# A decoder trunk on one core: the sums of the first two inner tiles' weights, and three low parts, move from VectorE to GpSimd

## The chip, the core and the metric

The kernel runs on one core of one Trainium2 chip. A core has a matrix engine (TensorE, PE in the profile, with its weight loads shown apart as PEld), VectorE (DVE), ScalarE (ACT), GpSimd (POOL) and SyncE (SP), which here only issues DMAs. Each engine takes its instructions strictly in order; what couples engines are semaphores that an instruction waits on before it starts. The metric is the device time of one execution in microseconds (us), as the median of several runs.

## The reference, cut to what matters

The reference is one inference step of a small decoder: one layer with a state-space mixer, one with differential attention, and after each of them a gated feed-forward network with a short convolution. The part that matters here is that network:

```python
def conv_ffn(x, buf, w_up, conv_w, conv_b, w_down):
    h = x @ w_up                               # (tokens, 1024) @ (1024, 5632)
    hp = jnp.concatenate([buf, h], axis=1)
    hc = conv_b + conv_w[0]*hp[:, 0:L] + conv_w[1]*hp[:, 1:1+L] + conv_w[2]*hp[:, 2:2+L]
    gate, val = jnp.split(hc, 2, axis=-1)
    return (gelu(gate) * val) @ w_down
```

It is computed for 1024 prompt tokens and 64 sample tokens together (1088 columns), once per layer, so twice in the program. Everything is float32, and the result has to be close to float32.

## The kernel before

**Three products for one.** A float32 operand is split in two: a high part, rounded by ScalarE (`A.copy`, line 144), and a low part, which is the operand minus the high part (line 145, VectorE). A product is then three matmuls, lines 809 to 811: high by high, low by high, high by low. `split_evac` (line 141) makes both parts. The names `whi` and `wlo` are the parts of weights, `xT_hi` and `xT_lo` those of the transposed activations.

**The up projection** is `ffn_up`, line 1090. It runs over 22 inner tiles f, each with 128 gate columns and 128 value columns of the weights. The first 768 tokens are multiplied by a scheme with seven products in place of eight (Strassen's, in Winograd's form), which needs sums of the weights' four quarters and sums of the activations' four quarters. `inputs(f)`, line 1099, prepares one inner tile: two DMAs bring the gate and the value weights into two `raw` tiles (line 1104), four sums s1 to s4 of 128 by 512 elements (lines 1109 to 1112) go into two `xr` tiles, and four calls of `split_evac` (line 1116) make the high and low parts of the gate weights, of the two `xr` tiles, and of the value weights. `raw` has two buffers and `xr` has two: the next inner tile's loads wait until the last reader of this one's `raw` tiles is done, and the first sums of a phase wait until the `xr` tiles of the phase before have been read.

**What comes ahead of it.** The activations of the up projection are made by the stage before it, tile of 128 tokens by tile: a residual addition (line 854), a second normalisation (line 864) with a Newton iteration on 128 by 1 elements for the inverse root (lines 120 to 134), then transposes on PE (line 870) and a `split_evac`. For three pairs of token tiles the sums of the activations (lines 911 to 914, `Combos.pair`) are made on VectorE before the transposes. The stage before is the gated output of the mixer (`glu`, first layer) or the attention's output projection (`o_proj`, second layer). So at the start of an up projection VectorE has the tail of the last stage and the head of the next at the same time.

**What sets the order.** The program is written in a straight line; a scheduler then orders each engine's instructions by an estimate of when each would be ready. The order so found is fixed when the program is built. SyncE's queue is in order too. Within a phase, the `acc` tiles (14 buffers) are used in turn, so a tile's first writer may have to wait for the last reader of an older one: in `inputs`, GpSimd clears two columns of each new `acc` tile (line 1121) and copies a few more (line 1122).

Of the kernel before, what the change touches and what calls it, by code (L numbers as in the profile page):

```python
# [10 lines left out]
F32 = mybir.dt.float32  # L11
# [4 lines left out]
ALU = mybir.AluOpType  # L16
# [57 lines left out]
def trunk_kernel(ctx, tc, I, O):  # L74
    nc = tc.nc
    V = nc.vector
    A = nc.scalar
    PE = nc.tensor
    GP = nc.gpsimd
    uid = [0]  # L80

    def nm(s):
        uid[0] += 1
        return f"{s}_{uid[0]}"
# [53 lines left out]
    xh = xpool.tile([P, KT, T], F32R, tag="xT_hi", name="xT_hi")  # L138
    xl = xpool.tile([P, KT, T], F32R, tag="xT_lo", name="xT_lo")

    def split_evac(hi_ap, lo_ap, ps_ap, scale=None):

        if scale is None:
            A.copy(hi_ap, ps_ap)  # L144
            V.tensor_tensor(lo_ap, ps_ap, hi_ap.bitcast(F32), ALU.subtract)  # L145
        else:
            A.mul(hi_ap, ps_ap, scale)
            V.scalar_tensor_tensor(lo_ap, ps_ap, scale, hi_ap.bitcast(F32), op0=ALU.mult, op1=ALU.subtract)
# [626 lines left out]
    def wslot(name, dtype=F32):  # L775

        c = pools["wc"] = (pools.get("wc", -1) + 1) % NWX
        return pools["w"].tile([P, 1024], dtype, tag=f"wx{c}", name=nm(name), bufs=1)
# [19 lines left out]
    def slot(tag, shape=None, dtype=F32):  # L798

        al = {"gx": "acc", "post": "acc", "junk": "gr"}  # L800
        shp, bufs = {"acc": ([P, 2 + SEQ + NB * 10], NACC), "gx": ([P, 4, 2 * P], NACC), "gr": ([P, 512], NGR),
                     "xr": ([P, D], 2), "junk": ([P, D], NGR), "post": ([P, D], NACC),
                     "cvo": ([P, 4, 18], 2), "cpar": ([P, 2 * NF, 20], 1), "ss": ([P, 1], 4)}[tag]
        tag = al.get(tag, tag)
        return pools["ph"].tile(shape or shp, dtype, tag=tag, name=nm(tag), bufs=bufs)
# [67 lines left out]
    def tail_b(y, tt, scale=None):  # L873

        t0, n = tokens(tt)
        for h in range(2):
            split_evac(xh[:, 4 * h : 4 * h + 4, t0 : t0 + n], xl[:, 4 * h : 4 * h + 4, t0 : t0 + n],
                       transposed(y[:, 512 * h : 512 * h + 512], n), scale)
# [6 lines left out]
    class Combos:  # L885
# [11 lines left out]
        def store(self, s, t, c0):  # L897
            k = 0
            while k < 4:
                n = min(3 - (4 * s + k) % 3, 4 - k)  # L900
                hi, lo = [self.view(s, part, k, n)[:, :, c0 : c0 + P] for part in range(2)]
                split_evac(hi, lo, t[:, k : k + n])
                k += n

        def pair(self, ya, yb, tt):

            t0 = tt * P
            tr = lambda y: transposed(y, P)
            t1, t2, t3, t4 = [slot("gr") for _ in range(4)]
            a, b = slice(0, 512), slice(512, D)  # L910
            V.tensor_tensor(t1, yb[:, a], ya[:, a], ALU.subtract)
            V.tensor_tensor(t3, yb[:, b], yb[:, a], ALU.subtract)
            V.tensor_tensor(t2, yb[:, b], t1, ALU.subtract)
            V.tensor_tensor(t4, ya[:, b], t2, ALU.subtract)
            split_evac(xh[:, 0:4, t0 : t0 + P], xl[:, 0:4, t0 : t0 + P], tr(t1))
            split_evac(xh[:, 4:8, t0 : t0 + P], xl[:, 4:8, t0 : t0 + P], tr(yb[:, b]))
            for s, t in enumerate((t2, t3, t4)):
                self.store(s, tr(t), t0 - HT)
# [171 lines left out]
    def ffn_up(i, down):  # L1090
# [8 lines left out]
        def inputs(f):  # L1099
            raws, hbs = [], []  # L1100
            for s in range(2):
                raw = pools["w"].tile([P, 1024], F32, tag="raw", name=nm("raw"), bufs=2)
                rv = u3(raw)
                nc.sync.dma_start(rv, wv[:, :, s * FF + f * P : s * FF + (f + 1) * P])
                raws.append(rv)
            a11, a12, a21, a22 = [r[:, 4 * k : 4 * k + 4] for r in raws for k in range(2)]
            s12, s34 = u3(slot("xr")), u3(slot("xr"))
            s1, s2, s3, s4 = [t[:, 4 * k : 4 * k + 4] for t in (s12, s34) for k in range(2)]
            V.tensor_tensor(s1, a21, a22, ALU.add)
            V.tensor_tensor(s2, s1, a11, ALU.subtract)  # L1110
            V.tensor_tensor(s3, a11, a21, ALU.subtract)
            V.tensor_tensor(s4, a12, s2, ALU.subtract)
            ws = []
            for r in (raws[0], s12, s34, raws[1]):
                hi, lo = u3(wslot("whi", F32R)), u3(wslot("wlo", F32R))
                split_evac(hi, lo, r)
                ws.append((hi, lo))
            for s in range(2):
                hb = slot("acc")
                hs = hb[:, 2 + SEQ :].rearrange("p (b r) -> p b r", r=10)  # L1120
                GP.memset(hb[:, 0:2], 0.0)
                GP.tensor_copy(hs[:, :, 0:2], cp[:, s * NF + f, 4:NPAR].rearrange("p (b r) -> p b r", r=2))
                hbs.append(hb)
            st[f] = ws, hbs, []
# [93 lines left out]


        inputs(0)  # L1220
        g = first(0)
        for _ in range(3):
# [8 lines left out]
        for f in range(NAHEAD, NF):  # L1231
            inputs(f)
            if f == NF - 1:
                down.begin()
            for s, _ in enumerate(first(f)):
                rest(f, s)
                conv(f, s)
            outputs(f)
# [865 lines left out]
```

## Time and profile before

| what | value |
|---|---|
| median of 3 runs | 2679.99 us (2677.94 to 2682.68) |
| the profiled execution | 2684.83 us, of which 2682.9 us are the span of the profile |
| busy share of PE, DVE, ACT, POOL | 93%, 73%, 47%, 24% |
| granted TensorE clock, mean | 0.976 of full speed |
| first up projection | about 436 to 930 us |
| second up projection | about 1906 to 2410 us |

A row of the page or of a timeline gives the start in us, the duration in us, the engine, the line, the operation, and what is written and read. Where an engine was idle ahead of the instruction, a bracket gives for how long and what released it. A row with "x2" at its end holds two instructions.

### The profile page before, as it was taken

The page shows a single profiled execution, that of the slowest core. Times are in us where ns is not written, and L with a number is a line of the kernel's source. Part 1 is how long each engine was busy: PE and PEld are TensorE (multiplying, and loading weights), DVE is VectorE, ACT ScalarE, POOL GpSimd, SP SyncE. Part 2 cuts the span into 40 slices and gives each one's busy share as a digit, 9 for nine tenths or more (in the row PEclk, how much of TensorE's full clock was granted, in tenths as well). Part 3 has the DMA queues.
Part 4 walks back from the last instruction along what each step waited for, and adds up shares of the span by engine and source line. Part 5 has one row for each costly group of instructions (what it writes and reads, how often), then busy time and mean ns, then how long its engine had stood idle before and what let it go on. Part 6 is the DMA issues. An engine that isn't in the chain of part 4 may idle for free.

```text
span 2682.9 us, 39622 instructions
## 1 busy us (share of the span) xinstructions
PE 2500.6 (93%) x14234; PEld 2203.5 (82%) x14234; DVE 1963.5 (73%) x3683; ACT 1270.9 (47%) x2559; POOL 657.3 (24%) x1062
## 2 busy tenths in 40 slices
PE   3778998999999989999999899989799999998997
PEld 2777887999999967778777788877699999996775
DVE  7994358777777789984232688875877777778999
ACT  6763334444444454354322677764544444444432
POOL 3220030111111175501201222113011111137661
PEclk9999998999999999999999899999899999999998
DMA  5443233222222233444646433335322222233334
GB/s 145 99 98 88 85 124 124 65 83 74 74 74 74 89 116 92 127 145 166 204 157 211 104 79 95 97 105 171 115 69 79 74 74 74 74 104 107 94 102 145
DMA packets 265688, 286.77 MB, mean 107 GB/s; under 512 B 42268, under 2 KB 212564, under 8 KB 265492
## 3 DMA queue, kind: packets, MB, share of 16 engines
q1 hardware_dynamic: 261892, 273.55, 33.0%
q0 software_dynamic: 3088, 9.77, 1.7%
q8 instruction: 113, 1.85, 0.3%
q10 hardware_dynamic: 512, 0.92, 0.1%
q14 instruction: 83, 0.68, 0.1%
HBM read 193.58 MB, written 70.93 MB: 99 GB/s over the span
## 4 chain that ended last, share of the span: by engine, by line
PE 58%; DVE 13%; DMA 4%; issue 3%; ACT 3%; POOL 2%; SPq 0%; DVEq 0%; POOLq 0%; ACTq 0%
PE mm L809 17%; PE mm L810 17%; PE mm L811 17%; DVE acc L1428 2%; DMA gr<-gd 1%; DVE xT_lo L145 1%; DVE S L1898 1%; PE mm L1417 1%; ACT S L1902 1%; DVE wst L145 1%; DVE xT_hi L145 1%; DVE acc L854 1%; PE mm L1436 1%; PE tr L870 1%; PE mm L1926 1%
## 5 line engine op out<-in xcount | busy, mean ns | idle before, releaser
L809 PE MATMUL mm<-xT_hi,whi 128*128 128x384 f32 (+1 forms) x1408 | 457.0, 325 | 2.0 <-ACT acc L1146 1.8
L810 PE MATMUL mm<-xT_lo,whi 128*128 128x384 f32 (+1 forms) x1408 | 456.3, 324 | 1.6 <-DVE xT_lo L145 1.6
L811 PE MATMUL mm<-xT_hi,wlo 128*128 128x384 f32 (+1 forms) x1408 | 454.2, 324 | 0.0
L809 PEld LDWEIGHTS mm<-xT_hi,whi 128*128 128x128 f32 x1408 | 265.4, 189 | 3.8 <-ACT acc L1146 2.4
L810 PEld LDWEIGHTS mm<-xT_lo,whi 128*128 128x128 f32 x1408 | 265.7, 189 | 2.4 <-DVE xT_lo L145 2.3
L811 PEld LDWEIGHTS mm<-xT_hi,wlo 128*128 128x128 f32 x1408 | 265.4, 189 | 0.8
L1195 POOL COPY cvo<-acc 128x2 f32<-128x2 f32 x88 | 53.3, 606 | 818.5 <-ACT acc L1178 818.5
L809 PE MATMUL mm<-whi,xT_hi 128*128 128x512 f32 x608 | 243.9, 404 | 4.9 <-ACT whi L792 4.7
L1192 DVE SCALAR_TENSOR_TENSOR acc<-acc,cpar,acc 128x1104 f32<-128x1104 f32 x176 | 240.0, 1385 | 4.7 <-ACT acc L1190 4.6
L810 PE MATMUL mm<-wlo,xT_hi 128*128 128x512 f32 x608 | 241.9, 398 | 0.1
L811 PE MATMUL mm<-whi,xT_lo 128*128 128x512 f32 x608 | 241.7, 399 | 0.0
L144 ACT CAST whi<-raw 128x1024 fp32r<-128x1024 f32 x88 | 92.5, 1051 | 253.5 <-PE mm L811 245.2
L1428 DVE TENSOR_TENSOR acc<-mm,acc 128x512 f32<-128x512 f32 x279 | 184.7, 680 | 9.8 <-PE mm L811 9.3
L145 DVE TENSOR_TENSOR wlo<-raw,whi 128x1024 fp32r<-128x1024 f32 x88 | 107.7, 1224 | 107.0 <-PE mm L810 91.6
L809 PE MATMUL mm<-acc,whi 128*128 128x384 f32 x528 | 179.1, 339 | 0.0
L811 PE MATMUL mm<-acc,wlo 128*128 128x384 f32 x528 | 178.7, 339 | 0.0
L810 PE MATMUL mm<-acc,whi 128*128 128x384 f32 x528 | 178.3, 338 | 0.0
L809 PEld LDWEIGHTS mm<-whi,xT_hi 128*128 128x128 f32 x608 | 115.6, 191 | 36.2 <-ACT whi L792 5.6
L810 PEld LDWEIGHTS mm<-wlo,xT_hi 128*128 128x128 f32 x608 | 114.7, 189 | 27.8 <-DVE wlo L793 0.8
L811 PEld LDWEIGHTS mm<-whi,xT_lo 128*128 128x128 f32 x608 | 114.4, 188 | 27.6 <-issue 0.8
L1190 ACT ACTIVATE acc<-acc,cpar 128x1104 f32<-128x1104 f32 x88 | 114.1, 1311 | 18.1 <-DVE acc L1161 11.9
L145 DVE TENSOR_TENSOR wlo<-xr,whi 128x1024 fp32r<-128x1024 f32 x88 | 107.6, 1223 | 16.7 <-ACT whi L144 8.6
(572 smaller groups left out, 6255.9 us busy)
## 6 DMA issues: line engine op xcount, KB each, us to landing
raw<-in_w_up_dram SPq DMA_DIRECT2D x88, 512.0 KB
gd<-acc SPq DMA_DIRECT2D x44, 552.0 KB
raw<-in_w_down_dram SPq DMA_DIRECT2D x44, 512.0 KB
gr<-gd SPq DMA_DIRECT2D x80, 256.0 KB
raw<-in_glu_w_dram SPq DMA_DIRECT2D x40, 256.0 KB
acc<-in_cache_k_dram SPq DMA_DIRECT2D x16, 512.0 KB
acc<-in_cache_v_dram SPq DMA_DIRECT2D x16, 512.0 KB
xj<-in_x_prompt_dram SPq DMA_DIRECT2D x8, 512.0 KB
```

Source lines behind the costliest of these rows:

```text
L144: A.copy(hi_ap, ps_ap)
L145: V.tensor_tensor(lo_ap, ps_ap, hi_ap.bitcast(F32), ALU.subtract)
L809: PE.matmul(out, lh, rh, start=start, stop=False, **kw)
L810: PE.matmul(out, lh, rl, start=False, stop=False, **kw)
L811: PE.matmul(out, ll, rh, start=False, stop=stop, **kw)
L854: V.scalar_tensor_tensor(y[:, hs], y[:, hs], r[0:n], xr[0:n, hs], op0=ALU.mult, op1=ALU.add)
L870: PE.transpose(ps[:, c * n : (c + 1) * n], y[:, c * P : (c + 1) * P], ident[0:n, 0:n])
L1190: A.activation(hc, hb[:, 2 : 2 + TG], AF.Identity, bias=cp[:, ft, 3:4], scale=cp[:, ft, 2:3])
L1192: V.scalar_tensor_tensor(hc, hb[:, tap : tap + TG], cp[:, ft, tap : tap + 1], hc, op0=ALU.mult, op1=ALU.add)
L1195: GP.tensor_copy(co[:, 0:2], hb[:, SEQ : SEQ + 2])
L1417: PE.matmul(pa[h], lt, wt[:, h * 512 : (h + 1) * 512], start=st and j == 0, stop=sp and j == len(seq) - 1)
L1428: V.tensor_tensor(a, ps, a, ALU.add)
```

## The change

For the first two inner tiles of each up projection the four sums of weights are given to GpSimd, and for the first inner tile three of the four low parts as well (those of the two sum tiles and of the value weights; the low part of the gate weights stays on VectorE). Both up projections have it, so 16 sums and 6 low parts move in all. No value that is computed changes, and the other 20 inner tiles are as before. The file grows by two lines, so that what is line 1109 before is line 1111 after, and so on from there; line 145 stays.

```diff
-    def split_evac(hi_ap, lo_ap, ps_ap, scale=None):
+    def split_evac(hi_ap, lo_ap, ps_ap, scale=None, on=V):
 
         if scale is None:
             A.copy(hi_ap, ps_ap)
-            V.tensor_tensor(lo_ap, ps_ap, hi_ap.bitcast(F32), ALU.subtract)
+            on.tensor_tensor(lo_ap, ps_ap, hi_ap.bitcast(F32), ALU.subtract)
...
-            V.tensor_tensor(s1, a21, a22, ALU.add)
-            V.tensor_tensor(s2, s1, a11, ALU.subtract)
-            V.tensor_tensor(s3, a11, a21, ALU.subtract)
-            V.tensor_tensor(s4, a12, s2, ALU.subtract)
+
+            E = GP if f < 2 else V
+            E.tensor_tensor(s1, a21, a22, ALU.add)
+            E.tensor_tensor(s2, s1, a11, ALU.subtract)
+            E.tensor_tensor(s3, a11, a21, ALU.subtract)
+            E.tensor_tensor(s4, a12, s2, ALU.subtract)
             ws = []
-            for r in (raws[0], s12, s34, raws[1]):
+            for j, r in enumerate((raws[0], s12, s34, raws[1])):
                 hi, lo = u3(wslot("whi", F32R)), u3(wslot("wlo", F32R))
-                split_evac(hi, lo, r)
+                split_evac(hi, lo, r, on=GP if f == 0 and j else V)
```

Since the scheduler orders all engines anew, instructions that the diff doesn't touch move too.

**VectorE and GpSimd, start of the first up projection.** raw_4230 and raw_4232 are the gate and value weights of the first inner tile, xr_4234 and xr_4235 its sums, raw_4503 and raw_4505 the weights of the second inner tile, gr_4291 to gr_4294 the activations' sums. VectorE before:

```order
L854 SCALAR_TENSOR_TENSOR acc_4136<-acc_4136,rr_4175,xr_4167 128x1024
L864 SCALAR_TENSOR_TENSOR acc_4071<-acc_4071,rr_4191,acc_2343 128x1024
L1111 TENSOR_TENSOR xr_4235<-raw_4230,raw_4232 128x512
L1112 TENSOR_TENSOR xr_4235<-raw_4230,xr_4234 128x512
L911 TENSOR_TENSOR gr_4291<-acc_4006,acc_3956 128x512
L912 TENSOR_TENSOR gr_4293<-acc_4006 128x512
L120 TENSOR_SCALAR rv_4218<-ss_4216 128x1
L913 TENSOR_TENSOR gr_4292<-acc_4006,gr_4291 128x512
L145 TENSOR_TENSOR wlo_4249<-xr_4235,whi_4248 128x1024
```

and now:

```order
L854 SCALAR_TENSOR_TENSOR acc_4136<-acc_4136,rr_4175,xr_4167 128x1024
L864 SCALAR_TENSOR_TENSOR acc_4071<-acc_4071,rr_4191,acc_2343 128x1024
L911 TENSOR_TENSOR gr_4291<-acc_4006,acc_3956 128x512
L912 TENSOR_TENSOR gr_4293<-acc_4006 128x512
L120 TENSOR_SCALAR rv_4218<-ss_4216 128x1
L913 TENSOR_TENSOR gr_4292<-acc_4006,gr_4291 128x512
L123 TENSOR_SCALAR rr_4220<-rv_4218 128x1
L914 TENSOR_TENSOR gr_4294<-acc_3956,gr_4292 128x512
```

What left VectorE stands on GpSimd, whose queue held only the two clears and two copies here:

```order
L145 TENSOR_TENSOR wlo_4253<-raw_4232,whi_4252 128x1024
L1111 TENSOR_TENSOR xr_4234<-raw_4232 128x512
L1112 TENSOR_TENSOR xr_4234<-xr_4234,raw_4230 128x512
L1123 MEMSET acc_4256 128x2
L1124 COPY acc_4256<-cpar_2673 128x8x2
L145 TENSOR_TENSOR wlo_4245<-xr_4234,whi_4244 128x1024
L1113 TENSOR_TENSOR xr_4235<-raw_4230,raw_4232 128x512
L1114 TENSOR_TENSOR xr_4235<-raw_4230,xr_4234 128x512
L1123 MEMSET acc_4259 128x2
L1124 COPY acc_4259<-cpar_2673 128x8x2
L145 TENSOR_TENSOR wlo_4249<-xr_4235,whi_4248 128x1024
```

The activations' sums now follow the normalisations with no weight work between, and GpSimd has eleven rows where it had four.

**ScalarE, the same place.** whi_4248 is the high part of xr_4235, whi_4513 that of the second inner tile's gate weights, acc_4259 the copy of the first product out of its accumulator, which PE waits for. Before:

```order
L144 CAST whi_4248<-xr_4235 128x1024
L144 CAST xT_hi<-tr_4299 128x4x128
L144 CAST whi_4513<-raw_4503 128x1024
L1146 COPY acc_4259<-mm_4262 128x384
L144 CAST xT_hi<-tr_4306 128x4x128
L144 CAST acc_3409<-tr_4313 128x3x128
```

and now:

```order
L144 CAST xT_hi<-tr_4299 128x4x128
L144 CAST whi_4248<-xr_4235 128x1024
L144 CAST xT_hi<-tr_4306 128x4x128
L1148 COPY acc_4259<-mm_4262 128x384
L144 CAST whi_4513<-raw_4503 128x1024
L144 CAST acc_3409<-tr_4313 128x3x128
```

The copy now stands ahead of the second inner tile's cast, but still behind the cast of xr_4235; the cast of the second inner tile stands ahead of acc_3409, the first activation sum.

**VectorE, start of the second up projection.** acc_18615 is a token tile whose second normalisation (L864) PE waits for; wlo_19052 is the low part of the second inner tile's gate weights, raw_19043 that tile's value weights. Before:

```order
L145 TENSOR_TENSOR wlo_19052<-raw_19041,whi_19051 128x1024
L134 SCALAR_TENSOR_TENSOR rr_18743<-rs_18742,rr_18743 128x1
L1109 TENSOR_TENSOR xr_19045<-raw_19043 128x512
L145 TENSOR_TENSOR acc_17917<-tr_18784,acc_17913 128x2x128
L130 SCALAR_TENSOR_TENSOR rs_18806<-rr_18807,rv_18805 128x1
L1111 TENSOR_TENSOR xr_19046<-raw_19041,raw_19043 128x512
L145 TENSOR_TENSOR acc_17917<-tr_18793,acc_17913 128x128
L864 SCALAR_TENSOR_TENSOR acc_18615<-acc_18615,rr_18743,acc_17778 128x1024
```

and now:

```order
L134 SCALAR_TENSOR_TENSOR rr_18743<-rs_18742,rr_18743 128x1
L130 SCALAR_TENSOR_TENSOR rs_18806<-rr_18807,rv_18805 128x1
L864 SCALAR_TENSOR_TENSOR acc_18615<-acc_18615,rr_18743,acc_17778 128x1024
L134 SCALAR_TENSOR_TENSOR rr_18807<-rs_18806,rr_18807 128x1
L145 TENSOR_TENSOR acc_17917<-tr_18784,acc_17913 128x2x128
L145 TENSOR_TENSOR wlo_19052<-raw_19041,whi_19051 128x1024
```

The normalisation that stood behind the low part of the second inner tile now stands ahead of it.

## The prediction

> **What bounds the kernel now.** First the page's span and busy times, then equal windows of 50 us (columns: window, its length, busy PE with its instructions, PEld, DVE, ACT, POOL, granted clock, DMA share, GB/s).
>
> ```profile
> span 2682.9 us, 39622 instructions
> PE 2500.6 (93%) x14234; PEld 2203.5 (82%) x14234; DVE 1963.5 (73%) x3683; ACT 1270.9 (47%) x2559; POOL 657.3 (24%) x1062
> ...
> 400.00:450.00 50.00, 39.50 (x195) 31.79 (x194) 44.85 (x121) 23.29 (x55) 3.39 (x8) 0.94 0.42 141
> 500.00:550.00 50.00, 50.00 (x305) 49.83 (x305) 37.56 (x43) 22.71 (x31) 4.36 (x16) 1.00 0.24 77
> 1900.00:1950.00 50.00, 37.41 (x203) 35.84 (x204) 42.79 (x102) 24.20 (x41) 5.50 (x12) 0.83 0.29 95
> ```
>
> Inside an up projection (500 to 550) PE is never idle, so that nothing is to be had there; at its two beginnings PE lacks 10.5 and 12.6 us of 50 and DVE is the fullest engine. Only there does the change count. What PE waits for, between 430 and 480 and between 1880 and 1960 (total, times, longest):
>
> ```profile
> PE tr L870 <- DVE gr L911: 9.7, 1, 9.7
> PE mm L809 <- ACT acc L1146: 1.1, 1, 1.1
> ...
> PE tr L870 <- DVE acc L864: 11.7, 2, 6.8
> ```
>
> So the instructions that matter are L911 in the first layer, L864 in the second, and L1146 between the halves of the first product. DVE ahead of L911:
>
> ```profile
> 433.79 1.23 DVE L145 TENSOR_TENSOR wlo<-raw,whi 128x1024 fp32r<-128x1024 f32 x1
> 436.21 0.69 DVE L145 TENSOR_TENSOR xT_lo<-tr,xT_hi 128x512 fp32r<-128x512 f32 x1
> 444.44 1.28 DVE L854 SCALAR_TENSOR_TENSOR acc<-acc,rr,xr 128x1024 f32<-128x1024 f32 x1
> 447.44 0.69 DVE L1112 TENSOR_TENSOR xr<-raw,xr 128x512 f32<-128x512 f32 x1
> 448.04 0.69 DVE L911 TENSOR_TENSOR gr<-acc,acc 128x512 f32<-128x512 f32 x1
> ```
>
> From 433.79 to 448.04 DVE runs without a pause. A sum costs it 0.60 (447.44 to 448.04), a low part about 1.2.
>
> **The price on POOL.** The same shapes on POOL elsewhere in this program (shortest, median, longest, in ns):
>
> ```profile
> L1298 POOL TENSOR_TENSOR xr<-raw,xr x36: 1286/1487/2328, 935.1 to 2601.9; 128x512 f32<-128x512 f32 x36
> L1804 POOL TENSOR_TENSOR qwl<-qraw,qwh x8: 2352/2369/2541, 1473.7 to 1701.2; 128x1024 fp32r<-128x1024 f32 x8
> ```
>
> So 1.29 a sum and 2.37 a low part, twice DVE's. POOL has room (3.39 and 5.50 of 50). But do the two engines run side by side?
>
> ```profile
> L134 DVE SCALAR_TENSOR_TENSOR rr<-rs,rr x204: 139/159/973, 8.6 to 2677.4; 128x1 f32<-128x1 f32 x69, 128x8 f32<-128x8 f32 x12, 128x2 f32<-128x2 f32 x12, 64x1 f32<-64x1 f32 x9
> ...
> 1209.91 1.89 POOL L791 TENSOR_TENSOR raw<-raw,kvg 128x1024 f32<-128x1024 f32 x1 [33.75 <-DMA raw<-in_w_k_dram]
> 1210.85 0.97 DVE L134 SCALAR_TENSOR_TENSOR rr<-rs,rr 128x1 f32<-128x1 f32 x1
> ...
> 955.14 4.44 POOL L1298 TENSOR_TENSOR xr<-raw 128x512 f32<-128x512 f32 x1 [4.37 <-DVE xT_hi L145]
> 956.15 1.28 DVE L145 TENSOR_TENSOR xT_hi<-xr,xT_hi 128x512 fp32r<-128x512 f32 x2
> ...
> 2601.91 1.49 POOL L1298 TENSOR_TENSOR xr<-raw,xr 128x512 f32<-128x512 f32 x1
> 2602.16 1.87 DVE L1428 TENSOR_TENSOR acc<-mm,acc 128x512 f32<-128x512 f32 x3
> ```
>
> They don't. At 1210.85 a DVE instruction whose line has a median of 0.16 lasts 0.97, its longest: until just the end of POOL's (1211.80). At 955.14 POOL's sum of 1.29 lasts 4.44 while DVE runs subtractions of two buffers in SBUF one behind another: POOL gets in when DVE pauses. At 2602.16 DVE reads `mm`, the accumulator, and three of them keep their 0.62 beside POOL's sum. I read: DVE with two sources in SBUF and POOL exclude each other; a DVE row with a source in the accumulator (L1428, xT_lo) doesn't.
>
> [...]
>
> **First layer.** Six of DVE's instructions ahead of L911 go: two low parts and four sums, 2 x 1.23 + 4 x 0.60 = 4.9; alone, L911 would start at 443.1. On POOL stand, ready in the same stretch, two low parts and two sums: 2 x 2.37 + 2 x 1.29 = 7.3. Two rows like that at 436.21 cover 1.4 of it, and 5.9 hold DVE. L911 comes at 448.04 - 4.9 + 5.9 = 449.0, 1.0 later. Lower bound: none holds it, -4.9.
>
> Now what is queued behind. The other two sums (L1111, L1112) write an `xr` tile that the last L854 still reads; that starts 3.6 before L911 in the rows above, 2.4 once the two sums between have gone, so it ends near 447.8. Then DVE has L864, L911 and L912 in a row, to 450.2, and POOL gets in at the small gap behind: 1.29, L913's 0.60, 1.29, so that L1112 ends near 453.5, where it was 448.1. On it hang, in this order, ACT's cast of that tile and (behind it in ACT's queue) the copy L1146 that PE waits for; and SP's load of the second tile.
>
> ```profile
> 448.87 1.09 PE L870 MATMUL tr<-ident,gr 128*128 128x128 f32 x4 [9.73 <-DVE gr L911]
> 452.81 0.69 PE L809 MATMUL mm<-xT_hi,whi 128*128 128x384 f32 x1 [1.14 <-ACT acc L1146]
> 457.40 0.42 PE L809 MATMUL mm<-acc,whi 128*128 128x384 f32 x1
> ...
> 451.33 1.04 ACT L144 CAST whi<-raw 128x1024 fp32r<-128x1024 f32 x1 [0.75 <-DMA raw<-in_w_up_dram]
> 452.29 0.47 ACT L1146 COPY acc<-mm 128x384 f32<-128x384 f32 x1
> ```
>
> ACT: cast 1.04, an xT_hi of half its size 0.5, copy 0.47: from 453.5 to 455.5, and PE goes on at 455.7 in place of 452.81: **+2.9**. The second tile's load, issued at L1112's end (447.60 before) and landing 3.7 later (451.33), lands near 457.2; its cast and that of the activation sum behind it end at 458.8, while PE asks for the latter at 455.7 + (457.40 - 452.81) = 460.3. It stays hidden with 1.5 to spare; without that cover each us of delay counts. Bounds of this layer: -4.9 (no exclusion at all) and +6.1 (each of the two sums takes 4.44, like that at 955.14).
>
> **Second layer.**
>
> ```profile
> 1905.81 1.94 PE L870 MATMUL tr<-ident,acc 128*128 128x128 f32 x8 [6.82 <-DVE acc L864]
> 1928.38 1.92 PE L870 MATMUL tr<-ident,acc 128*128 128x128 f32 x8 [4.84 <-DVE acc L864]
> 1933.17 1.07 PE L870 MATMUL tr<-ident,acc 128*128 128x128 f32 x8
> ...
> 1917.02 0.69 DVE L1112 TENSOR_TENSOR xr<-raw,xr 128x512 f32<-128x512 f32 x1
> 1922.80 1.05 ACT L144 CAST whi<-raw 128x1024 fp32r<-128x1024 f32 x1 [3.19 <-DMA raw<-in_w_up_dram]
> 1923.88 1.23 DVE L145 TENSOR_TENSOR wlo<-raw,whi 128x1024 fp32r<-128x1024 f32 x1 [2.72 <-ACT whi L144]
> 1926.95 1.28 DVE L864 SCALAR_TENSOR_TENSOR acc<-acc,rr,acc 128x1024 f32<-128x1024 f32 x1
> ```
>
> Up to the middle the exchange is as above: a low part at 2.37 for 1.23, mostly beside DVE's work, +0.7 at the first gap, then two sums at 1.29 for 0.60, +1.4, and +0.4 of another low part: PE is 2.5 late. The second gap, 4.84, is of another kind: L864 stood in DVE's queue behind the second inner tile's low part, which idled 2.72 for ACT's cast, which idled 3.19 for the DMA. In the new order L864 stands ahead of it. So PE, which came free at 1928.38 - 4.84 = 1923.5, comes at 1926.0 and goes straight on: -2.4. The next token tile's L864 is now the one behind that low part. POOL's L1112, held by the clear of `acc` and by DVE, ends near 1921 (1917.7 before); load 5.1 (1917.7 to 1922.80), cast 1.05, low part 1.23, a little of DVE's other work, L864: about 1930.3. These transposes start at 1930.4 in place of 1933.17: **-2.8**. Bounds: -4.84 - 1.1 (both waits go, the six sums cost nothing) and +2.5 (the second gap only moves).
>
> **Clock.** After the gap:
>
> ```profile
> 1928.00:1931.00 3.00, 2.62 (x11) 2.65 (x12) 3.00 (x8) 2.05 (x3) 0.00 (x0) 0.57 0.00 0
> 1931.00:1934.00 3.00, 3.00 (x19) 2.70 (x18) 2.78 (x6) 0.16 (x1) 0.00 (x0) 0.86 0.59 175
> ...
> 2423.30:2425.70 2.40, 0.00 (x1) 0.00 (x0) 2.40 (x5) 0.00 (x0) 2.40 (x1) 0.99 0.91 267
> 2427.00:2430.00 3.00, 3.00 (x8) 2.32 (x8) 1.80 (x2) 1.48 (x3) 2.92 (x3) 0.50 0.66 204
> ```
>
> The 4.84 cost 3 x 0.43 + 3 x 0.14 = 1.7 more in clock. A stall of about 1.4 stays in my account (1929.0 to 1930.4), shorter than the 2.40 that still cost the clock at 2423; I credit half, **-0.9**.
>
> [...]
>
> **Sum**, against the profiled execution's own 2684.83: +2.9 - 2.8 - 0.9 = -0.8, 2684.0; this execution lies 4.84 above the median, so about **2679** in the median's terms. A measurement of this kernel can tell some 0.2% (5.4 us) from no change, so below 2674.6 is faster and above 2685.4 slower.
>
> **Rivals.**
> A, the engines hardly hold each other: DVE finishes its head early. For it: POOL is nearly empty, and much of DVE here is 128 by 1 work between dependent steps, with gaps that POOL can use; against it, 1210.85. First layer -4.4, second -4.84 - 1.7 - 1.1 = -7.6: 2668.
> B, slower: the two late sums starve. Each waits for a pause of DVE as at 955.14 (4.44 - 1.29 = 3.2); L1112 ends at 447.8 + 2 x 4.44 = 456.7, ACT's cast holds L1146 and PE goes on 6.1 later; in the second layer the same 3 us push the load and eat the 2.8, and the gap with its clock stays: 2686. It decides when L1112 ends after 456; from 454.3 on the sum turns to a loss. For it, those 4.44; against it, that DVE's row here has 128 by 1 pauses.
> C, nothing comes of it, because the waits for DMA and ACT set both places whatever DVE does: 2680. For it, the bracket at 1922.80; against it, the 9.7 for L911.
>
> **Chances.** Forecast 0.43, A 0.31, B 0.21, C 0.05. The forecast's own range, from its bounds, is 2673 to 2686: of its 0.43, 0.03 lies below 2674.6 and 0.03 above 2685.4; of B 0.04 lies within. So faster 0.31 + 0.03 = 0.34; slower 0.17 + 0.03 = 0.20; no change 0.46. For 8 in 10 the range reaches to both rivals: 2668 to 2687.
>
> **What will show it.** First layer: the gap ahead of L870 ends near 450, the second half of the product starts near 455.7, the late sum ends near 453.5, and rows of DVE with two SBUF sources (L130, L134, L854) are longer where POOL works. Second layer: no 4.84 ahead of `tr` at 1926, and the last token tile's transposes at 1930.4. I am wrong by A if DVE's rows keep their lengths beside POOL's and L911 comes near 444; by B if `whi` or the load is PE's last releaser past 456; altogether if PE's idle time changes outside these two beginnings.

## The result

The changed kernel takes 2689.81 us (median of 7 runs, 2686.83 to 2694.56); the kernel before, on the same chip, 2682.45 us (7 runs, 2677.86 to 2685.75). The ratio is 1.0031, with a 95% interval of 1.0022 to 1.0040: slower by some 8 us (the two medians are 7.4 apart). The prediction was 2679 and "no change" as the likeliest, with 2687 as the upper end of its range. The sign is that of rival B, the mechanism is not.

**The profile after.** Busy times, then the 50 us windows of the two beginnings (columns as before):

```profile
PE 2497.0 (93%) x14234; PEld 2200.9 (82%) x14234; DVE 1973.5 (73%) x3661; ACT 1271.1 (47%) x2559; POOL 663.0 (25%) x1084
...
400.00:450.00 50.00, 37.63 (x181) 29.79 (x180) 46.75 (x114) 23.42 (x52) 14.41 (x11) 0.87 0.46 153
1900.00:1950.00 50.00, 35.71 (x186) 33.41 (x185) 43.57 (x86) 21.38 (x40) 21.23 (x17) 0.83 0.32 105
```

VectorE has 22 instructions fewer and is busy for longer: 1973.5 us, where it was 1963.5. In the first window it went from 44.85 to 46.75 with some operations gone. The rows below show why: a row's duration contains the time for which GpSimd holds the instruction up (L911 at 443.80 lasts 1.75, and 0.69 before), so the work that left came back as waiting. What PE waits for, in the windows 430 to 480 and 1880 to 1960:

```profile
PE tr L870 <- DVE gr L911: 7.3, 1, 7.3
PE mm L810 <- DVE xT_lo L145: 3.3, 1, 3.3
PE mm L810 <- DVE acc L145: 1.7, 1, 1.7
...
PE tr L870 <- DVE rr L134: 6.9, 1, 6.9
PE mm L809 <- ACT acc L144: 3.2, 1, 3.2
PE tr L870 <- DVE rr L123: 3.0, 1, 3.0
```

The stall of 4.84 us in the second layer has gone, as forecast, and so has that for L1146 in the first. In their place stand three new ones: 1.7, 3.0 and 3.2. Two lines need care. The 3.3 for xT_lo (0.3 before) stands right ahead of the 7.3 in PE's queue; together they are 10.6, where it was 10.0 before, so most of it has only moved from one to the other. And the 6.9 put down to L134 is the old 6.8 for L864: L864 ends at 1907.04, a short L134 right behind it at 1907.18, and PE goes on at 1907.19.

**First layer, by rows.** GpSimd, VectorE and PE of the changed kernel:

```profile
429.63 2.38 POOL L145 TENSOR_TENSOR wlo<-raw,whi 128x1024 fp32r<-128x1024 f32 x1 [31.64 <-DVE rr L134]
442.77 2.24 POOL L1113 TENSOR_TENSOR xr<-raw,raw 128x512 f32<-128x512 f32 x1 [2.06 <-DVE acc L854]
444.97 1.72 POOL L1114 TENSOR_TENSOR xr<-raw,xr 128x512 f32<-128x512 f32 x1
452.81 1.28 POOL L1113 TENSOR_TENSOR xr<-raw,raw 128x512 f32<-128x512 f32 x1
...
429.46 2.56 DVE L130 SCALAR_TENSOR_TENSOR rs<-rr,rv 128x1 f32<-128x1 f32 x2
443.80 1.75 DVE L911 TENSOR_TENSOR gr<-acc,acc 128x512 f32<-128x512 f32 x1
452.90 1.20 DVE L134 SCALAR_TENSOR_TENSOR rr<-rs,rr 128x1 f32<-128x1 f32 x1
...
445.70 1.09 PE L870 MATMUL tr<-ident,gr 128*128 128x128 f32 x4 [7.33 <-DVE gr L911]
450.18 0.67 PE L809 MATMUL mm<-xT_hi,whi 128*128 128x384 f32 x1
458.13 0.44 PE L810 MATMUL mm<-acc,whi 128*128 128x384 f32 x1 [1.74 <-DVE acc L145]
```

A Newton step on 128 by 1 elements, 0.15 us alone, lasts until GpSimd's low part or sum beside it ends: two of them 2.56 beside the low part at 429.63, one 1.20 beside the sum at 452.81. L911, 0.69 before, lasts 1.75, since GpSimd's L1113 has its turn first, up to 445.01. The stall of 1.74 is the low part of an activation sum, which stands behind the Newton steps that the second tile's sums hold.

**Second layer, by rows.** PE, then VectorE and GpSimd:

```profile
1915.90 1.09 PE L870 MATMUL tr<-ident,gr 128*128 128x128 f32 x4 [3.03 <-DVE rr L123]
1918.90 0.69 PE L809 MATMUL mm<-xT_hi,whi 128*128 128x384 f32 x1 [0.20 <-ACT acc L1148]
1922.49 0.34 PE L809 MATMUL mm<-acc,whi 128*128 128x384 f32 x1
1927.59 0.60 PE L870 MATMUL tr<-ident,acc 128*128 128x128 f32 x4
1932.35 0.66 PE L809 MATMUL mm<-acc,whi 128*128 128x384 f32 x1 [3.19 <-ACT acc L144]
1936.02 1.03 PE L870 MATMUL tr<-ident,acc 128*128 128x128 f32 x8
...
1913.50 2.26 DVE L911 TENSOR_TENSOR gr<-acc,acc 128x512 f32<-128x512 f32 x1
1925.74 2.35 DVE L134 SCALAR_TENSOR_TENSOR rr<-rs,rr 128x1 f32<-128x1 f32 x1
1928.35 2.05 DVE L145 TENSOR_TENSOR wlo<-raw,whi 128x1024 fp32r<-128x1024 f32 x1
1930.32 1.21 DVE L130 SCALAR_TENSOR_TENSOR rs<-rr,rv 128x1 f32<-128x1 f32 x1
...
1912.87 2.34 POOL L145 TENSOR_TENSOR wlo<-xr,whi 128x1024 fp32r<-128x1024 f32 x1 [1.16 <-DVE rv L120]
1924.88 3.19 POOL L145 TENSOR_TENSOR wlo<-xr,whi 128x1024 fp32r<-128x1024 f32 x1 [3.37 <-ACT whi L144]
1929.28 2.24 POOL L1113 TENSOR_TENSOR xr<-raw,raw 128x512 f32<-128x512 f32 x1
```

The stall of 3.03 is L911 waiting out the low part at 1912.87. The stall of 3.19 is the low part of an activation sum that stood behind three held rows: a Newton step at 1925.74, 2.2 us longer than alone beside the first inner tile's last low part (1924.88), and 1928.35 and 1930.32, some 0.8 and 1.0 longer beside the second inner tile's sums.

### The profile page after: what moved, and what is told of

Same layout as the page of the kernel before. It is cut to its first block, busy times and chain, and to the rows that moved or that the text cites. A ratio compares the mean times of both kernels' runs of the same rounds, so it can differ in the third digit from the quotient of the medians.

```text
span 2687.6 us, 39649 instructions
## 1 busy us (share of the span) xinstructions
PE 2497.0 (93%) x14234; PEld 2200.9 (82%) x14234; DVE 1973.5 (73%) x3661; ACT 1271.1 (47%) x2559; POOL 663.0 (25%) x1084
## 4 chain that ended last, share of the span: by engine, by line
PE 63%; DVE 19%; DMA 5%; ACT 5%; issue 4%; POOL 3%; SPq 0%; DVEq 0%; ACTq 0%; POOLq 0%
PE mm L809 18%; PE mm L810 18%; PE mm L811 18%; DMA gr<-gd 2%; DVE acc L1430 2%; DVE xT_lo L145 2%; DVE S L1900 1%; POOL rs L126 1%; DVE acc L854 1%; ACT S L1904 1%; DVE xT_hi L145 1%; PE mm L1419 1%; PE mm L1928 1%; PE mm L1438 1%; DVE wst L145 1%
## 5 line engine op out<-in xcount | busy, mean ns | idle before, releaser
L1900 DVE CUSTOM_DVE_ANT_0 S<-mm,tb 128x512 f32<-128x512 f32 (+3 forms) x192 | 101.5, 552 | 22.4 <-PE mm L1898 18.9
```

The lines of the kernel that those rows point to most:

```text
L1900: V.tensor_tensor_reduce(S_[j][:, k0 : k0 + w], ps[:, 0:w], H["tb"][:, b0 : b0 + w], 0.125, -3e38, ALU.add, ALU.max, mx[:, j, c : c + 1])
```

## The experiments

The profiles all hold 14,234 matrix instructions, so the time at which PE starts its nth can be compared between them, whatever the order of the rest. The table gives, worked out from the traces, how long PE takes from its 2077th to its 3169th (399.7 to 599.6 us in the first profile of the kernel before: the first beginning), from the 10173rd to the 10726th (1889.7 to 1999.7: the second), in between, and from there to its last. The ratio is to the kernel before, with its 95% interval.

| kernel | ratio | first beginning | between | second beginning | behind it |
|---|---|---|---|---|---|
| before, the first profile | | 199.9 | 1290.2 | 110.0 | 667.6 |
| before, again | | 198.4 | 1289.7 | 110.1 | 667.6 |
| the change | 1.0031 [1.0022, 1.0040] | 203.8 | 1292.5 | 112.2 | 668.7 |
| first projection only | 1.0017 [1.0008, 1.0025] | 204.4 | 1286.6 | 110.6 | 668.2 |
| second projection only | 1.0015 [1.0006, 1.0024] | 199.4 | 1289.0 | 111.9 | 668.5 |
| memsets in place of reads | 1.0005 [0.9996, 1.0013] | 192.9 | 1294.5 | 102.7 | 678.4 |
| memsets, again | | 192.4 | 1293.7 | 103.6 | 680.2 |
| moved work left out | 0.9975 [0.9964, 0.9985] | 194.0 | 1297.8 | 104.1 | 669.3 |
| change, Newton steps with one source | 1.0014 [1.0005, 1.0023] | 200.7 | 1287.7 | 110.3 | 666.5 |
| before, Newton steps with one source | 1.0044 [1.0031, 1.0057] | 200.4 | 1287.4 | 110.7 | 675.3 |
| sums only | 1.0021 [1.0012, 1.0029] | 200.8 | 1292.9 | 107.9 | 667.7 |
| low parts only | 1.0034 [1.0023, 1.0045] | 203.3 | 1295.8 | 111.8 | 667.7 |
| second projection, first tile only | 1.0011 [1.0002, 1.0019] | 198.5 | 1292.3 | 110.9 | 669.5 |
| second projection, second tile's sums only | 1.0011 [1.0001, 1.0020] | 198.3 | 1289.8 | 113.1 | 670.0 |
| one low part only | 1.0009 [0.9999, 1.0018] | 198.2 | 1289.3 | 111.5 | 668.7 |
| three raw buffers, ten slots | 0.9961 [0.9948, 0.9974] | 197.5 | 1289.8 | 107.0 | 665.3 |
| the change, three raw buffers, ten slots | 1.0006 [0.9996, 1.0015] | 201.3 | 1286.4 | 117.5 | 665.2 |
| ten slots | 1.0001 [0.9992, 1.0010] | 198.3 | 1287.6 | 107.0 | 670.8 |

Where its order is as before, the first beginning takes 198.2 to 199.9 in six profiles, and the second 110.0 to 110.6 in three: a single profile is good to about 1.7 and 0.6 us. Between them the six profiles whose order is as before up to the second beginning lie from 1289.0 to 1292.3.

### Each projection by itself

```diff
-            E = GP if f < 2 else V
+            E = GP if f < 2 and i == 0 else V
...
-                split_evac(hi, lo, r, on=GP if f == 0 and j else V)
+                split_evac(hi, lo, r, on=GP if f == 0 and j and i == 0 else V)
```

> The change in the first up projection only. Theory L, from the traces (there the change's execution goes from 4.9 us ahead at the row L864 to 0.9 ahead after the beginning): 3 to 5 us above the kernel before. If the difference of the medians is from elsewhere: within 1 us.

The same with `i == 1`:

> The change in the second up projection only. Theory L, from the traces (1.3 us behind at L2025, 4.8 behind after the beginning): 2.5 to 4.5 us above the kernel before. By the prediction as made: 3.7 below.

Measured 1.0017 and 1.0015, some 4 us each; together that is the loss of the whole change. The first beginning is 4.5 to 6.2 us longer than in the six profiles with its order unchanged, the second 1.3 to 1.9 than in the three. So there is a loss in both beginnings. In the second the profile shows less than the median (1.9 of 4.0, whose interval begins at 1.6). The prediction of -3.7 for the second (-2.8, and -0.9 of clock) is refuted by a run of its own.

### The exclusion: memsets in place of reads

```diff
-            E.tensor_tensor(s1, a21, a22, ALU.add)
...
+            if f < 2:
+                for s, p, q in ((s1, a21, a22), (s2, s1, a11), (s3, a11, a21), (s4, a12, s2)):
+                    GP.tensor_tensor(s[:, :, 0:1], p[:, :, 0:1], q[:, :, 0:1], ALU.subtract)
+                    for _ in range(3):
+                        GP.memset(s, 0.0)
```

and the three low parts alike.

> Each of the 22 moved operations is replaced on GpSimd by the same operation on a 128 by 4 or 128 by 8 slice (so that it waits for the same data) and three memsets of its whole tile, which take longer than the operation (three of 0.46 or 0.92 us by the two memsets of 128 by 1024 in 1.84) but read nothing; the sums and low parts are left out. Theory L (GpSimd's reads and VectorE's two-source operations exclude each other, and that exclusion is the loss): the loss goes, VectorE's rows keep their lengths, 4 to 12 us below the kernel before. Rival O (GpSimd's results come late, or the new order of the rows is bad): the loss stays, 4 to 9 us above the kernel before.

At the two beginnings theory L holds, by more than its own upper end: 192.9 and 102.7, that is 7.0 and 7.3 us below the first profile of the kernel before, and 5.5 and 7.4 below the second. GpSimd is as busy, and VectorE doesn't notice:

```profile
431.42 2.98 POOL L148 MEMSET wlo<- 128x1024 f32 x3
431.19 0.35 DVE L130 SCALAR_TENSOR_TENSOR rs<-rr,rv 128x1 f32<-128x1 f32 x2
```

Two Newton steps take 0.35 beside a memset; beside the low part at 429.63 of the changed kernel two took 2.56. The wait of PE for the pair sums (L916 here), 7.3 in the changed kernel, falls to 3.7:

```profile
PE tr L875 <- DVE gr L916: 3.7, 1, 3.7
```

But the median is that of the kernel before, not 4 to 12 us below: 10.8 us are given back behind the second beginning (678.4 against 667.6). To see whether that was the single execution, the kernel was profiled once more:

> The kernel with memsets in place of the moved operations, one more profile: its gain of 6.8 and 4.9 us at the two beginnings stays within 1 us if it belongs to the order and the lack of exclusion; what is given back in the second down projection (7.8 us) stays if it belongs to the order there, and goes if it was the single execution.

By the table's marks the gains are 7.5 and 6.4 us, within 1 us of the 7.0 and 7.3 of its first profile (the 6.8, 4.9 and 7.8 of the expectation aren't taken at these marks), and 680.2 stays too. So the loss behind belongs to this kernel's order, which differs in the later tiles of the second up projection and in the down projection behind it. Which row does it was not found.

### What VectorE's relief is worth

```diff
-            s12, s34 = u3(slot("xr")), u3(slot("xr"))
+            s12, s34 = raws if f < 2 else (u3(slot("xr")), u3(slot("xr")))
...
-            on.tensor_tensor(lo_ap, ps_ap, hi_ap.bitcast(F32), ALU.subtract)
+            if on is not GP:
+                on.tensor_tensor(lo_ap, ps_ap, hi_ap.bitcast(F32), ALU.subtract)
```

Beside this the four sums stand under `if f >= 2`, and the first tile's four products share the one low part that is made.

> The 22 moved operations are left out on both engines (the first two tiles use the raw weights in place of the sums, and the first tile one low part for all). It bounds what VectorE's relief is worth. Theory L: 5 to 14 us below the kernel before, a little more than with memsets. Rival O (order): near the kernel with the change, 3 to 9 us above the kernel before. Rival C (VectorE is not what PE waits for): within 2 us of the kernel before.

0.9975, 6.7 us by the ratio, and 5.9 us at each beginning by the profile. It gives 7.6 us back between the two, where its order differs from that of before in the attention as well (near 1204 to 1237 and 1780 to 1795); whether that order does it was not tried. The beginnings refute rival C: VectorE is what PE waits for. The change turns a relief worth 6 us at each place into a loss.

### Is it the second source?

```diff
-                V.scalar_tensor_tensor(s[p], r[p], r[p], v[p], op0=ALU.mult, op1=ALU.mult)
+                V.tensor_scalar(s[p], r[p], r[p], v[p], op0=ALU.mult, op1=ALU.mult)
+                V.tensor_scalar(r[p], s[p], 1.5, r[p], op0=ALU.add, op1=ALU.mult)
+                continue
```

> The kernel with the change, and the Newton steps on 128 by 1 elements rewritten so that each has one tensor source (the other factors as per-partition scalars); the values are the same. Theory L (it is the second source in SBUF that makes VectorE and GpSimd exclude each other, and Newton steps waiting out a GpSimd operation are most of the loss): those rows keep about 0.15 us beside GpSimd's sums, and 3 to 7 us of the 8.3 come back (0.998 to 0.999 of the kernel with the change). Rival O (late results and order): the time stays within 2 us of the kernel with the change, 6 to 10 us above the kernel before.

```profile
433.55 2.38 POOL L147 TENSOR_TENSOR wlo<-raw,whi 128x1024 fp32r<-128x1024 f32 x1 [31.39 <-DVE rr L131]
447.93 1.71 POOL L1116 TENSOR_TENSOR xr<-raw,xr 128x512 f32<-128x512 f32 x1
433.72 0.33 DVE L131 TENSOR_SCALAR rr<-rs,rr 128x1 f32<-128x1 f32 x2
448.44 2.28 DVE L866 SCALAR_TENSOR_TENSOR acc<-acc,rr,acc 128x1024 f32<-128x1024 f32 x1
```

It is. With one tensor source two Newton steps take 0.33 beside a low part of 2.38, while L866, which still has two, lasts 2.28 in place of 1.28. The beginnings fall to 200.7 and 110.3, near those of the kernel before, and the ratio to 1.0014 from 1.0031: about half of the loss is gone. The control:

> The same rewriting of the Newton steps in the kernel before, as a control. Theory L: little, since GpSimd reads almost nothing at the two beginnings there: within 3 us of the kernel before. If the rewritten steps are faster by themselves, this falls as much as the run above.

The rewritten steps aren't faster by themselves. The control lost 12 us, outside what was expected, and not at the beginnings: 7.7 us lie behind the second, where it has another order. This makes the difference between the two runs useless as a size; the rows above carry the verdict on the second source, and how much of the loss is Newton steps stays open.

### Which operations

```diff
-                split_evac(hi, lo, r, on=GP if f == 0 and j else V)
+                split_evac(hi, lo, r, on=V)
```

> Only the 16 sums move, the low parts stay on VectorE. Theory L, by GpSimd's time with reads (16 sums of 1.29 are 21 us, 6 low parts of 2.37 are 14 us) weighted by where they lie: 3 to 6 us above the kernel before. Rival A': if it is the long low parts that do the harm, within 2 us.

and, with `E = V` in place of the other line,

> Only the 6 low parts move, the sums stay. Theory L: 2 to 5 us above the kernel before; a Newton step beside a low part lasts up to 2.4 us. If it is the sums alone: within 1 us, or a gain, since a low part is 1.2 us of VectorE.

Measured 1.0021 and 1.0034. Both are in the ranges or over them, and they don't add up: by themselves the two halves lose 14.7 us, together 8.3. By the table the low parts cost most at the beginnings (203.3 and 111.8, against 200.8 and 107.9), but the medians hold more than the beginnings, in particular for the sums: with these alone the two beginnings together are 1.2 us shorter than in the first profile of before, and the median is 5.6 us longer. The low parts' 9.1 are 5.2 at the beginnings and 5.6 between them. So at the beginnings rival A' is the nearer one, and where the sums lose their 5.6 us is not shown. I read that a wait of 1.2 or 2.4 us in a chain of 128 by 1 steps (1.20 at 452.90, 2.35 at 1925.74 in the change) is drawn anew with every order, and that such pieces aren't terms of a sum.

### The second layer's stalls

First inner tile only (`f == 0 and i == 1` in both lines), and the second inner tile's four sums only (`f == 1 and i == 1`, no low parts):

> Second up projection only, first inner tile only (four sums, three low parts on GpSimd); the second inner tile's sums stay on VectorE. If the failing step is the stall ahead of the pair sums (3.03 us at 1915.90 with the change, L911 held by the first tile's low part), that stall is here too: 2 to 4 us above the kernel before. If it is the late stall (3.19 at 1932.35, behind the second tile's sums): within 1.5 us.

> Second up projection only, second inner tile's four sums only. The other half: if the late stall decides, 1.5 to 3 us above the kernel before; if the early one, within 1.5 us or a gain, as no stall ahead of the pair sums.

PE in the kernel with the first tile's work moved:

```profile
1913.49 0.63 PE L870 MATMUL tr<-ident,gr 128*128 128x128 f32 x4 [2.21 <-DVE rr L123]
1928.74 0.66 PE L809 MATMUL mm<-acc,whi 128*128 128x384 f32 x1 [2.55 <-DVE rr L134]
```

and in that with the second tile's sums moved:

```profile
1925.13 1.94 PE L870 MATMUL tr<-ident,acc 128*128 128x128 f32 x8 [6.21 <-DVE acc L864]
```

Each half costs about as much as the other (1.0011 both), so neither stall decides alone. The first tile's work makes both stalls by itself, somewhat shorter, so the late one doesn't need the second tile's sums: its last low part on GpSimd holds a Newton step of VectorE (2.34 at 1922.79 in that kernel). With the second tile's sums alone the old stall ahead of L864 is still there, at 6.21 for 4.84.

### One low part, and the load behind it

```diff
+            E = V
...
-                split_evac(hi, lo, r, on=GP if f == 0 and j else V)
+                split_evac(hi, lo, r, on=GP if f == 1 and i == 1 and j == 0 else V)
```

> The kernel before with one single operation on GpSimd: the low part of the second inner tile's gate weights in the second up projection, behind which L864 stood (4.84 us of PE). Order theory: the stall goes or shrinks to 2 us, for one exclusion of at most 2.4 us: 2 to 5 us below the kernel before. If exclusion eats it: within 2 us.

```profile
1917.21 2.63 DVE L1111 TENSOR_TENSOR xr<-raw 128x512 f32<-128x512 f32 x1 [2.76 <-DMA raw<-in_w_up_dram]
1916.95 2.34 POOL L145 TENSOR_TENSOR wlo<-raw,whi 128x1024 fp32r<-128x1024 f32 x1 [7.82 <-ACT whi L144]
1921.65 1.94 PE L870 MATMUL tr<-ident,acc 128*128 128x128 f32 x8 [4.83 <-DVE acc L864]
```

1.0009, no gain, and the stall is 4.83, as it was. The next row in VectorE's queue waits for the same tile's load (2.76), and then waits out the low part on GpSimd (2.63 for 0.69). So the load seems to be what comes late, which a third buffer for the raw weights should mend; a weight slot pays for its room. The `raw` tag serves four other places of the program, which get the third buffer too:

```diff
-                raw = pools["w"].tile([P, 1024], F32, tag="raw", name=nm("raw"), bufs=2)
+                raw = pools["w"].tile([P, 1024], F32, tag="raw", name=nm("raw"), bufs=3)
...
-    NWX = 11
+    NWX = 10
```

> The kernel before with three buffers in place of two for the raw weights (and one weight slot fewer, 10 in place of 11), so that a next tile's load needn't wait for the last reader: nothing moves between engines. If the wait for the second tile's load is what makes the 4.84 us stall: 2 to 5 us below the kernel before. If VectorE's work itself sets the time there: within 2 us.

0.9961, 10 us below the kernel before, twice what was expected, and faster than both kernels; the stall of 4.84 is gone. (The first wait for L864 stays, 6.68 at 1899.00 for 6.82; it is put down to L134, which ends just behind L864.) But the cause isn't settled by that, as the control shows:

> Control for the three buffers: two raw buffers as before, ten weight slots in place of eleven. If the third raw buffer makes the gain: not faster than the kernel before (0 to 6 us above it). If the new order by itself makes it: 5 to 10 us below.

Ten slots with two buffers give no gain in the median (1.0001), yet in its profile the second beginning is 107.0 too, and the stall of 4.84 is gone as well. So the third buffer, with the order that comes of it, makes the gain, and not, or not only, where it was looked for. Then the change on top of it:

> The change on top of three raw buffers and ten weight slots. Theory L: exclusion costs here too, 3 to 9 us above the kernel with three buffers, so 2674 to 2680. If the loss of the change came from the wait for the second tile's load (pushed behind GpSimd's late sums), which three buffers take away: within 2 us of the kernel with three buffers, near 2671.

1.0006: the change costs some 12 us here, more than without, and more than the 3 to 9 expected. PE's waits between 1880 and 1970, in the kernel with three buffers:

```profile
PE tr L870 <- DVE rr L134: 8.1, 2, 6.7
```

and with the change on top:

```profile
PE tr L870 <- DVE rr L123: 12.8, 1, 12.8
...
1891.11 2.50 DVE L130 SCALAR_TENSOR_TENSOR rs<-rr,rv 128x1 f32<-128x1 f32 x2
```

An early load doesn't take the loss away. The change's own profile says the same: its second tile's first sum waits 0.57 for the load in the first layer (451.57) and not at all in the second (1928.04), so a late load isn't what the change loses by. But this run doesn't show that its 12 us are exclusion: in the 12.8 us of waiting, which end with L864 at 1903.80, VectorE has one held row, that of 1891.11, some 2.2 us. The rest of the difference from 6.7 goes with another order there, and what the 12 us are stays open.

### How far one execution goes

> The kernel before, one more profile: how far do two executions of one and the same order lie apart outside the beginnings? If the places near 213 to 252, 1340 and 1740 to 1765, where the change's profile differs from the first by 2 to 5 us though the order is the same, are matters of the single execution: they move here too, and the two beginnings keep their length within 1 us. If they belong to the change: all marks within 1 us of the first profile.

The second profile of the kernel before is 1.5 us shorter at the first beginning (198.4), more than the 1 us expected, and 0.1 longer at the second; other places move by 1 to 4 us between two executions of one order. One of them, a place in the attention where the change alters no row, in the first profile of the kernel before:

```profile
1743.52 3.20 POOL L1870 TENSOR_TENSOR kh<-qraw,kh 128x1024 fp32r<-128x1024 f32 x1 [5.59 <-ACT kh L1869]
1743.19 1.28 DVE L1912 SCALAR_TENSOR_TENSOR S<-S,cc,S 128x1024 f32<-128x1024 f32 x1
```

and in that of the change:

```profile
1740.51 2.42 POOL L1872 TENSOR_TENSOR kh<-qraw,kh 128x1024 fp32r<-128x1024 f32 x1 [5.07 <-ACT kh L1871]
1740.71 3.31 DVE L1914 SCALAR_TENSOR_TENSOR S<-S,cc,S 128x1024 f32<-128x1024 f32 x1
```

In these two profiles the one that starts first goes through: there GpSimd comes 0.33 us later and waits (3.20 for 2.4), here it comes 0.20 earlier and VectorE waits (3.31 for 1.28). The second profile of the kernel before goes like that of the change here, so this difference isn't the change's.

## Why the prediction was wrong

**What bounds the kernel:** right in the main. A loss shows in both beginnings (two runs of their own), and VectorE is the engine (the run with the work left out, 5.9 us shorter at each).

**Exclusion by the second source in SBUF:** right, and now shown by the change's rows (two Newton steps take 2.56 beside the low part at 429.63), by the memsets (two take 0.35) and by the Newton steps with one source (two take 0.33).

**"POOL gets in when DVE pauses":** wrong, and this is the step that failed. I read 955.14, where GpSimd waited 3.2 us, as the rule, and asked how late GpSimd's results would be. The profile before had a counterexample 7 us earlier:

```profile
948.45 2.33 POOL L1298 TENSOR_TENSOR xr<-raw,xr 128x512 f32<-128x512 f32 x1
949.58 1.75 DVE L145 TENSOR_TENSOR xT_hi<-raw,xT_hi 128x512 fp32r<-128x512 f32 x1
```

There GpSimd waited for the end of one VectorE instruction, at 949.65, and the next one, 0.68 alone, waited for GpSimd. In the changed kernel each moved operation waits for one instruction of VectorE at most: 2.24 for 1.29 at 442.77, 1.72 at 444.97, and 3.19 for a low part of 2.35 at 1924.88. So the late sum ended earlier than I forecast. Moved to this profile by the lead of 4.8 us with which it enters (L1038's first issue at 406.78 for 411.59), my forecast for that end was 448.7; it ended at 446.7. The late results were not the matter: at L1148, which hangs on them, PE waits 0.20 (1918.90) in the second layer and not at all in the first. The cost falls on the other engine. As I read the rows, a chain of 128 by 1 steps on VectorE leaves a gap behind each step, GpSimd takes it with a whole sum or low part, and the next step of 0.15 waits 1.2 to 2.4 us. I counted such gaps as GpSimd's chance and, in rival B, as what speaks against a loss.

**First layer, +2.9:** 3.9 against the first profile, near 5 against the mean of the six. L911's transposes come at +1.6 (445.70, with the lead of 4.8; forecast +1.0), the second half of the product at +2.2 (450.18; forecast +2.9). The load that the forecast has "issued at L1112's end (447.60 before)" is the first of two, at L1111's end (L1112 ends at 448.1); nothing hung on that. The rest is the stall of 1.74 at 458.13, which I had covered with "1.5 to spare": I looked at the cast of the second tile there, while it was the low part of an activation sum, behind Newton steps that the second tile's four sums held.

**Second layer, -2.8:** measured +2.2 in the profile and 1.0015 in its own run. The profile enters the place 1.3 us behind (the transposes at 1896.89 for 1895.60). The first gap is +0.1 (forecast +0.7), and the gap of 4.84 is gone: PE is at the next token tile at 1927.59, 2.1 us ahead by that measure (forecast -2.4). Then the term fails: the last token tile's transposes come at 1936.02, +1.6 and not -2.8. I had put "a little of DVE's other work" there. The first tile's last low part and the second tile's four sums lie on GpSimd just then, and I had charged VectorE nothing for waiting on them; the three held rows ahead of the stall of 3.19 lose 2.2, 0.8 and 1.0. This is where the failed step shows in the sum: the term is off by 4.4 us.

**Clock, -0.9:** wrong with it, since the stalls weren't gone but new. The window before:

```profile
1915.00:1920.00 5.00, 4.38 (x29) 4.11 (x28) 5.00 (x13) 4.25 (x9) 0.86 (x2) 1.00 0.55 188
```

and after:

```profile
1915.90:1919.00 3.10, 2.89 (x13) 2.50 (x13) 3.10 (x7) 1.70 (x4) 1.07 (x3) 0.50 0.00 0
```

Behind the stall of 3.03 the clock is 0.50 and the half product that follows takes 3.59 (1918.90 to 1922.49), where it took 2.22 before (1916.09 to 1918.31). The row at 2423 on which this term rests stands shortly behind a wait of 3.40 that ended at 2419.70, behind which the clock was 0.50 already (2421.00 to 2423.00), which I hadn't said. Ahead of the stall of 3.03 the clock was back (1.00 from 1912.00 to 1912.87), and 0.50 followed all the same.

**Rivals.** A named the right price under a false condition: with nothing excluded the beginnings give 12 to 14 us, where I had 12; the match of the size is luck, since the engines do hold each other (2.56 for two Newton steps at 429.46). B had the sign and not the mechanism: it let GpSimd starve, and VectorE did. The chance of 0.20 for slower was too small since both the forecast and B made GpSimd the one that waits.

## What to carry to other kernels

By the rows of this case, work that moves from VectorE to GpSimd is taken off VectorE without a wait if what runs beside it is a VectorE instruction with one tensor source (0.33 for two beside a low part) or a source in the accumulator (0.62 each at 2602.16), or if GpSimd only writes (0.35 for two beside a memset). Otherwise ask what VectorE runs meanwhile: two long independent instructions lost one wait each (L911 and L912 at 443.80 and 445.48, 1.75 for 0.69), but a chain of tiny dependent ones can lose a whole GpSimd instruction at each step (1.20 at 452.90). Price such a move from the rows of both engines, and look at the median and at the same place in a second profile before you credit a single stall of 2 us.

## What the runs showed of the hardware

- At one and the same place of one order the granted clock came back at different times: behind the stall ahead of L911 (9.73 and 9.75 us) it was 0.50 up to 457 in the first profile of the kernel before, and 0.99 from 449 to 454 in the second, so that the half product took 4.01 us there (452.81 to 456.82) and 2.20 here (450.21 to 452.41). The second profile, PE and then the window:

```profile
446.02 1.09 PE L870 MATMUL tr<-ident,gr 128*128 128x128 f32 x4 [9.75 <-DVE gr L911]
450.21 0.44 PE L809 MATMUL mm<-xT_hi,whi 128*128 128x384 f32 x1 [1.40 <-ACT acc L1146]
...
449.00:454.00 5.00, 3.79 (x23) 3.76 (x24) 4.86 (x10) 3.09 (x7) 0.00 (x0) 0.99 0.09 28
```

  The first profile's window:

```profile
449.00:454.00 5.00, 3.86 (x16) 3.46 (x17) 5.00 (x10) 3.08 (x6) 0.31 (x2) 0.50 0.68 202
```

  What sets the time at which the clock comes back is shown by no run.
- What gives GpSimd its turn isn't settled: it waited for one VectorE instruction at the moved operations of the changed kernel (2.24 for 1.29 at 442.77) and at 948.45 (2.33), and for several at 955.14 (4.44).
- Per-partition scalars that come from SBUF don't count as a second source here: of the one-source Newton steps L130 has two of them and L131 one, and beside the low part at 433.55 they keep 0.27 (433.96) and 0.33 for two (433.72).
